# Low parts of the first feed-forward's weights kept in DRAM between the two halves of the sequence

## The chip, the core and the metric

The kernel runs on one NeuronCore of a Trainium2 chip. It is measured in device microseconds per launch. Work is spread over TensorE (PE: matrix products, with PEld its weight loads), VectorE (DVE), ScalarE (ACT), GpSimd (POOL) and SyncE (SP), which here issues nearly all DMAs. Each engine takes its own instructions strictly in order and waits on semaphores of the others.

## The reference

Two layers over 1024 tokens of width 1024, in float32. Layer 0 mixes tokens with attention and pooling, layer 1 with an RWKV-7 recurrence; each is followed by a SwiGLU feed-forward of inner width 2816:

```python
x = x + y                                   # y: the layer's mixer
x = x + (silu(h @ w_gate) * (h @ w_up)) @ w_down   # h = rmsnorm(x)
```

The change concerns only the feed-forward of layer 0 (`w_gate`, `w_up`, `w_down`: 22 blocks of 128 columns each).

## The kernel before

Activations are held transposed, in two halves of 512 tokens. Every float32 weight is split in two: `hi` is the value rounded to the matmul format (a ScalarE copy), `lo = raw - hi` (a VectorE subtract). A product is three matmuls: hi by hi, hi by the activation's lo, lo by hi (`mm3`, lines 163 to 165).

`load_part` (line 142) does this for one part of 128x512 numbers, 256 KB: a DMA on SP into one of two `wraw` buffers (line 150), the copy into `whi` (line 151), the subtract into `wlo` (line 152). `whi` and `wlo` have five buffers each. A raw buffer comes free once its subtract is done, a `whi` or `wlo` buffer once TensorE has used it. So SP's third load waits for the first part's subtract, and ScalarE's sixth copy for the first part's last matmul. One part feeds 12 matmuls of 128x512.

`ffn` (line 683) runs over blocks of 128 inner columns: gate (2 parts), up (2 parts), and behind each group of four blocks the down projection (8 parts, one for each 128 output columns; 4 for the last group of two). One half takes 88 + 44 = 132 parts. A gate's result leaves its PSUM buffer through ScalarE and the VectorE multiply at line 726 (half 1) and an up's at line 732; in half 1 there are two such buffers ("fm").

The layer-0 feed-forward runs once for half 0 (`g0` and line 1367) and once for half 1 (`f1`, line 1369), and each run loads and splits the same weights. In half 0 it stands alone. In half 1 it is filler: 96 matmuls run ahead, and the rest is woven into two `job` calls of the recurrence on half 0. A job first prepares four pairs of heads (many VectorE products into `ZL`, `XR`, `bk`, small matmuls on TensorE), then inverts 32x32 triangles on VectorE alone (30 steps of `pd` and `nu`, lines 1110 and 1112, then transposes of 2 us into `t` and `XR`, lines 1120 and 1118), and then runs eight steps over 64 tokens each. Between these pieces `weave` takes a fixed number of filler matmuls (`rw.fr`: 6, 5, 16, 7, ...), and a scheduler orders every engine's list once, when the program is built. During the jobs SP also loads and stores the recurrence's own tiles (lines 961, 1053, 985).

Of the kernel before, what the change touches and what calls it, by code (L numbers as in the profile page):

```python
# [9 lines left out]
F32 = mybir.dt.float32  # L10
# [6 lines left out]
P = 128  # L17
# [3 lines left out]
HN = 512  # L21
# [59 lines left out]
def rd(ap):  # L81
    return ap.bitcast(F32)


def setup(ctx, tc, k):
    nc = tc.nc
    k.tc, k.nc = tc, nc
    k.const = ctx.enter_context(tc.tile_pool(name="const", bufs=1))
    k.uid = 0
    k.prio, k.cur = {}, 0  # L90
    k.cc = k.const.tile([P, NCC], F32, tag="cc", name="cc")
    k.cv = k.const.tile([P, NCV], F32, tag="cv", name="cv")

    k.eps = k.const.tile([P, 64], F32, tag="eps", name="eps")
    nc.gpsimd.memset(k.eps[:, 0:1], RMS_EPS)
    nc.gpsimd.memset(k.eps[:, 1:2], GN_EPS)
    nc.gpsimd.memset(k.eps[:, 2:3], 1e-35)
    k.hlast = k.const.tile([P, KT], F32, tag="hlast", name="hlast")
    k.om = k.const.tile([P, 48], F32, tag="om", name="om")
    k.nb = k.const.tile([P, 16], F32, tag="nb", name="nb")  # L100
    k.bones = k.const.tile([P, P], F32R, tag="bones", name="bones")
    k.lag2, k.lag3 = 100000, 100000
# [30 lines left out]
    return k.ps.tile([P, HN], F32, tag=tag, name=nm(k, tag), bufs=bufs)  # L133


def load_w(k, ap, tag="w", w=512, bufs=None, pool=None):

    p, n = ap.shape
    return [load_part(k, ap[:, c:c + min(512, n)], p, min(512, n), tag, w, bufs, pool) for c in range(0, n, 512)]


def load_part(k, ap, p, n, tag="w", w=512, bufs=None, pool=None):
    hi, lo = ((pool or k.wp).tile([P, w], F32R, tag=tag + i, name=nm(k, tag + i), bufs=bufs or k.wbufs) for i in ("hi", "lo"))
    raw = k.wp.tile([P, 512], F32, tag="wraw", name=nm(k, "wraw"), bufs=k.rawbufs)
    dst = raw[0:p, 0:n]
    if len(ap.shape) == 3:
        dst = dst.rearrange("p (a b) -> p a b", b=ap.shape[2])
    elif len(ap.shape) == 4:
        dst = dst.rearrange("p (a b c) -> p a b c", b=ap.shape[2], c=ap.shape[3])
    k.nc.sync.dma_start(dst, ap)  # L150
    k.nc.scalar.copy(hi[0:p, 0:n], raw[0:p, 0:n])  # L151
    k.nc.vector.tensor_tensor(lo[0:p, 0:n], raw[0:p, 0:n], rd(hi[0:p, 0:n]), ALU.subtract)  # L152
    return hi, lo


# [34 lines left out]
def run(gen):  # L190

    while True:
        try:
            next(gen)
        except StopIteration as e:
            return e.value


def chain(*gens):
    for g in gens:  # L200
        yield from g
# [478 lines left out]
        out[kt] = part(k, pair(k, *acc), t)  # L680


def ffn(k, ins, L, halves, H, X, acc, tp, groups, after=None, silu=True, fb0=0):
    nc = k.nc

    def project(w):
        o = {half: pmm(k) for half in halves}
        for c in range(2):
            for half in halves:
                yield from mm3(k, o[half], [(blk(w, kt), H[half][kt]) for kt in range(4 * c, 4 * c + 4)], c == 0, c == 1)  # L690
        return o

    def down(n, fb0, acts, last):
        per = max(1, 4 // n)
        cur = None
        for half, m in [(half, m) for half in halves for m in range(8)] if last else [(half, m) for m in range(8) for half in halves]:
            if cur != m // per:
                cur = m // per
                w = []
                for f in range(0, n, 4):  # L700
                    c = min(4, n - f)
                    w.append(load_part(k, ins[f"wd{L}"][per * cur:per * cur + per, :, fb0 + f:fb0 + f + c].rearrange("m p f c -> p m f c"), P, per * c * P))
            o = pmm(k)
            yield from mm3(k, o, [(blk(w, (m % per) * n + i), acts[fb0 + i, half]) for i in range(n)])
            nc.vector.tensor_tensor(X[half][m], o, X[half][m], ALU.add)  # L705
            if last:
                after(half, m)
# [3 lines left out]
    for gi, n in enumerate(groups):  # L711
        acts, sgs = {}, {}
        for fb in range(fb0, fb0 + n):
            g = yield from project(load_w(k, ins[f"wg{L}"][fb]))
            for half in halves:
                sg = sgs[half] = tp.tile([P, HN], F32, tag="nt", name=nm(k, "sg"), bufs=k.ntbufs)
                if silu:
# [8 lines left out]
                    nc.vector.tensor_tensor(sg, g[half], sg, ALU.mult)  # L726
            yield from behind
            behind = iter(())
            u = yield from project(load_w(k, ins[f"wu{L}"][fb]))
            for half in halves:  # L730
                sg = sgs[half]
                nc.vector.tensor_tensor(sg, u[half], sg, ALU.mult)
# [503 lines left out]
def build(ctx, tc, ins, outs, dbg=None, stop=99):  # L1236
    nc = tc.nc
    k = K()
# [5 lines left out]
    H = [[None] * KT for _ in range(2)]  # L1244
    X = [[None] * KT for _ in range(2)]
# [60 lines left out]
    c_m, mp = pool("m1", "right")  # L1306
    c_t, tp = pool("t1", "right")
# [28 lines left out]
    c_u, u = pool("u")  # L1336
# [20 lines left out]

    GP, G0, G1, G2 = ((4,),(),(4,4,4,4,2),(4,4,4,4,2))
    n = sum(GP) + sum(G0)
    g0 = ffn(k, ins, 0, (0,), H, X, U, tp, GP)  # L1360
    ahead(g0, 24)
    for m in MO[1][NP:]:
        on[1].add(X[1][m])
    run(g0)
    make_h(k, on[1], "ffn0", X[1], M, H[1])
    run(ffn(k, ins, 0, (0, 1), H, X, U, tp, G0, fb0=sum(GP)))
    run(ffn(k, ins, 0, (0,), H, X, U, tp, G1, after0, True, n))
    rw.ln_exp, rw.mx, rw.wl_bufs, k.sigm = False, U, 2, True
    f1 = chain(ffn(k, ins, 0, (1,), H, X, M, mp, GP, silu=None), ffn(k, ins, 0, (1,), H, X, M, mp, G2, after0, None, n))
    f1 = using(k, f1, mm=(pf, "fm", 2), ntbufs=3)  # L1370
    lead, share = (96, 0)
    ahead(f1, lead)
# [178 lines left out]
```

## Time and profile before

| | us |
|---|---|
| median of 3 runs | 2699.88 (2699.42 to 2700.76) |
| the profiled execution | 2699.79 |
| its span, first to last instruction | 2698.0 |
| TensorE busy | 2632.5 |
| VectorE busy | 1725.1 |
| ScalarE busy | 1298.7 |

Half 0 of the layer-0 feed-forward lies at about 500 to 850 us, the dense projections of the recurrence at 880 to 1060, the first job at 1060 to 1280 (its VectorE-heavy start until 1180), the second at 1280 to 1500, and the end of the half-1 feed-forward at 1500 to 1560. A 128x512 matmul shows 0.39 us in the trace, but they are pipelined: one starts every 0.22 to 0.23 us. "Idle before" is the time an engine stood still, with the instruction whose end let it go on.

### The profile page before, as it was taken

The numbers are of one execution on the slowest core, as the hardware profiler recorded it, in microseconds if no ns is written. First come the engines' busy times: TensorE is split into PE (matmuls) and PEld (weight loads), VectorE is DVE, ScalarE is ACT, GpSimd is POOL, SyncE is SP. The second block draws the span as 40 slices with busy tenths as digits, with TensorE's granted clock in tenths as the row PEclk, the third lists the DMA queues.
The fourth block names the chain that finished last, engine by engine and source line by source line (L and its number), as shares of the span: only waits on it lengthen the run. The fifth ranks groups of instructions, "written<-read, shape, count | busy, mean of one in ns | idle before, by whom it ended". The sixth has DMA issues, their size and how long they took to land.

```text
span 2698.0 us, 40269 instructions
## 1 busy us (share of the span) xinstructions
PE 2632.5 (98%) x15368; PEld 2072.6 (77%) x15368; DVE 1725.1 (64%) x2940; ACT 1298.7 (48%) x2297; POOL 49.4 (2%) x139
## 2 busy tenths in 40 slices
PE   8999999999999999999999999999999999999999
PEld 6787878788888777777777677777777777888887
DVE  8777684653446655975995676469778856534443
ACT  7555564443224766434634467664445444332232
POOL 1000000000001000000000000000000000000000
PEclk9999999999999999999999999999999999999999
DMA  4111131233333545424433534554244336333333
GB/s 136 58 51 57 42 98 48 83 96 98 96 96 113 172 161 189 129 83 131 148 91 99 195 94 160 168 179 128 87 138 140 92 97 202 101 98 96 97 97 94
DMA packets 170529, 306.11 MB, mean 113 GB/s; under 512 B 18896, under 2 KB 26192, under 8 KB 170336
## 3 DMA queue, kind: packets, MB, share of 16 engines
q1 hardware_dynamic: 156512, 278.38, 33.5%
q10 hardware_dynamic: 13824, 25.17, 2.5%
q8 instruction: 120, 1.97, 0.3%
q14 instruction: 73, 0.60, 0.1%
HBM read 257.04 MB, written 46.43 MB: 112 GB/s over the span
## 4 chain that ended last, share of the span: by engine, by line
PE 77%; DVE 14%; ACT 3%; DMA 3%; issue 3%; SPq 0%; DVEq 0%; ACTq 0%
PE mm L163 16%; PE mm L164 16%; PE mm L165 16%; PE fm L163 6%; PE fm L164 5%; PE fm L165 5%; DVE wlo L152 2%; PE mm L175 1%; DVE nu L1112 1%; DVE pd L1110 1%; DVE ZL L1068 1%; DMA wraw<-in_wd_dram 1%; DMA wraw<-in_wu_dram 1%; ACT whi L151 1%; PE o L1177 1%
## 5 line engine op out<-in xcount | busy, mean ns | idle before, releaser
L151 ACT CAST whi<-wraw 128x512 fp32r<-128x512 f32 x738 | 454.0, 617 | 886.8 <-PE mm L164 484.5
L152 DVE TENSOR_TENSOR wlo<-wraw,whi 128x512 fp32r<-128x512 f32 x738 | 501.3, 683 | 446.0 <-ACT whi L151 436.4
L163 PE MATMUL mm<-hh,whi 128*128 128x512 f32 x864 | 343.7, 400 | 6.7 <-ACT hh L355 6.2
L165 PE MATMUL mm<-hh,wlo 128*128 128x512 f32 x864 | 338.7, 392 | 0.0
L164 PE MATMUL mm<-hl,whi 128*128 128x512 f32 x864 | 337.8, 392 | 0.0
L163 PE MATMUL mm<-uh,whi 128*128 128x512 f32 x728 | 283.5, 391 | 0.9 <-DVE x L1318 0.9
L165 PE MATMUL mm<-uh,wlo 128*128 128x512 f32 x728 | 283.1, 389 | 1.2 <-DVE wlo L152 1.2
L164 PE MATMUL mm<-ul,whi 128*128 128x512 f32 x728 | 283.2, 390 | 0.0
L163 PE MATMUL fm<-h1h,whi 128*128 128x512 f32 x528 | 218.7, 415 | 14.8 <-DVE sg L726 10.6
L165 PE MATMUL fm<-h1h,wlo 128*128 128x512 f32 x528 | 208.7, 396 | 0.5 <-DVE wlo L152 0.5
L164 PE MATMUL fm<-h1l,whi 128*128 128x512 f32 x528 | 208.5, 395 | 0.1
L163 PEld LDWEIGHTS mm<-hh,whi 128*128 128x128 f32 x864 | 162.5, 188 | 43.1 <-ACT hh L355 6.9
L165 PEld LDWEIGHTS mm<-hh,wlo 128*128 128x128 f32 x864 | 162.7, 188 | 34.8 <-DVE wlo L152 0.6
L164 PEld LDWEIGHTS mm<-hl,whi 128*128 128x128 f32 x864 | 162.9, 189 | 32.7 <-DVE hl L260 1.3
L163 PE MATMUL fm<-hh,whi 128*128 128x512 f32 x416 | 172.4, 414 | 3.5 <-ACT hh L259 2.8
L164 PE MATMUL fm<-hl,whi 128*128 128x512 f32 x416 | 164.5, 396 | 0.2 <-DVE hl L260 0.2
L165 PE MATMUL fm<-hh,wlo 128*128 128x512 f32 x416 | 164.6, 396 | 0.0
L163 PEld LDWEIGHTS mm<-uh,whi 128*128 128x128 f32 x728 | 136.5, 188 | 34.6 <-issue 2.7
L164 PEld LDWEIGHTS mm<-ul,whi 128*128 128x128 f32 x728 | 136.6, 188 | 31.1 <-issue 1.1
L165 PEld LDWEIGHTS mm<-uh,wlo 128*128 128x128 f32 x728 | 136.7, 188 | 30.0 <-DVE wlo L152 2.0
L705 DVE TENSOR_TENSOR x<-mm,x 128x512 f32<-128x512 f32 x96 | 66.2, 692 | 119.8 <-PE mm L165 119.6
L163 PEld LDWEIGHTS fm<-h1h,whi 128*128 128x128 f32 x528 | 99.5, 189 | 48.7 <-DVE sg L726 13.3
(338 smaller groups left out, 4632.4 us busy)
## 6 DMA issues: line engine op xcount, KB each, us to landing
wraw<-in_wg_dram SPq DMA_DIRECT2D x176, 256.0 KB, 2.8
wraw<-in_wu_dram SPq DMA_DIRECT2D x176, 256.0 KB, 2.7
wraw<-in_wd_dram SPq DMA_DIRECT2D x176, 256.0 KB, 2.7
wraw<-in_w_in_dram SPq DMA_DIRECT2D x52, 256.0 KB, 2.9
x<-in_xT_dram SPq DMA_DIRECT2D x32, 256.0 KB, 4.8
x<-x SPq DMA_DIRECT2D x32, 256.0 KB, 3.1
wraw<-in_w_k_dram SPq DMA_DIRECT2D x32, 256.0 KB, 2.9
wraw<-in_w_v_dram SPq DMA_DIRECT2D x32, 256.0 KB, 3.0
```

Of the source, the lines that this page charges most:

```text
L151: k.nc.scalar.copy(hi[0:p, 0:n], raw[0:p, 0:n])
L152: k.nc.vector.tensor_tensor(lo[0:p, 0:n], raw[0:p, 0:n], rd(hi[0:p, 0:n]), ALU.subtract)
L163: nc.tensor.matmul(out, wh, xh, start=(first and i == 0), stop=False)
L164: nc.tensor.matmul(out, wh, xl, start=False, stop=False)
L165: nc.tensor.matmul(out, wl, xh, start=False, stop=(last and i == n - 1))
L175: k.nc.tensor.matmul(out[n * q:n * q + n], w[:, n * j:n * j + n], xs[j], start=c == 0, stop=c + g == len(xs), tile_position=(0, n * q))
L705: nc.vector.tensor_tensor(X[half][m], o, X[half][m], ALU.add)
L1068: nc.vector.tensor_tensor(ZL[h][HS[1 - h], i, bs], s4[HS[1]], self.msk[HS[1]].rearrange("p a t -> p (a t)").unsqueeze(1).broadcast_to([64, ...
L1110: nc.vector.tensor_tensor(pv, nu[:, j + 1:32, j:j + 1].broadcast_to([P, n, j]), nu[:, j:j + 1, 0:j].broadcast_to([P, n, j]), ALU.mult)
L1112: nc.vector.tensor_tensor(nu[:, j + 1:32, 0:j], nu[:, j + 1:32, 0:j], pv, ALU.add)
L1177: nc.tensor.matmul(sp[HS[h], i], BK[h][:, i, c], uv[h][:, i], start=True, stop=True)
```

## The change

For the layer-0 feed-forward a part now has a key (layer, matrix, block, column). When half 0 makes a part's `lo`, a DMA on SP stores it in a DRAM tile of its own (new line 160). When half 1 loads the same part, the raw weights still come in and ScalarE still copies `hi`, but `lo` comes by a second DMA on SP from that DRAM tile (new line 155), and no subtract is issued.

```diff
@@ load_w, load_part @@
-    return [load_part(k, ap[:, c:c + min(512, n)], p, min(512, n), tag, w, bufs, pool) for c in range(0, n, 512)]
+    return [load_part(k, ap[:, c:c + min(512, n)], p, min(512, n), tag, w, bufs, pool, key and f"{key}_{c}") for c in range(0, n, 512)]
...
     k.nc.sync.dma_start(dst, ap)
     k.nc.scalar.copy(hi[0:p, 0:n], raw[0:p, 0:n])
+    if key in k.low:
+        k.nc.sync.dma_start(rd(lo[0:p, 0:n]), k.low[key][0:p, 0:n])
+        return hi, lo
     k.nc.vector.tensor_tensor(lo[0:p, 0:n], raw[0:p, 0:n], rd(hi[0:p, 0:n]), ALU.subtract)
+    if key is not None:
+        k.low[key] = k.dram.tile([P, HN], F32, tag="lo" + key, name="lo" + key)
+        k.nc.sync.dma_start(k.low[key][0:p, 0:n], rd(lo[0:p, 0:n]))
     return hi, lo
@@ ffn @@
+    key = lambda *a: "_".join(map(str, (L,) + a)) if keep else None
...
-            g = yield from project(load_w(k, ins[f"wg{L}"][fb]))
+            g = yield from project(load_w(k, ins[f"wg{L}"][fb], key=key("g", fb)))
...
-            u = yield from project(load_w(k, ins[f"wu{L}"][fb]))
+            u = yield from project(load_w(k, ins[f"wu{L}"][fb], key=key("u", fb)))
@@ build @@
-    g0 = ffn(k, ins, 0, (0,), H, X, U, tp, GP)
+    g0 = ffn(k, ins, 0, (0,), H, X, U, tp, GP, keep=True)
...
-    run(ffn(k, ins, 0, (0,), H, X, U, tp, G1, after0, True, n))
+    run(ffn(k, ins, 0, (0,), H, X, U, tp, G1, after0, True, n, True))
...
-    f1 = chain(ffn(k, ins, 0, (1,), H, X, M, mp, GP, silu=None), ffn(k, ins, 0, (1,), H, X, M, mp, G2, after0, None, n))
+    f1 = chain(ffn(k, ins, 0, (1,), H, X, M, mp, GP, silu=None, keep=True), ffn(k, ins, 0, (1,), H, X, M, mp, G2, after0, None, n, True))
```

The down projection's parts get a key ("d") in the same way. Line numbers below the new code grow by 8 to 10. Over the program SP's list grows from 1072 to 1336 rows (132 stores and 132 loads more), VectorE's shrinks by 136, of which 132 are subtracts.

On SP in the middle of half 0, in the third group of blocks, stood only the raw loads, each waiting for a subtract on VectorE (`DVE_49`):

```order
L150 DMA wraw_5665<-in_wu_dram 128x512 [waits DMAHW1_49,DVE_49]
L150 DMA wraw_5671<-in_wu_dram 128x512 [waits DMAHW2_49,DVE_49]
L150 DMA wraw_5707<-in_wg_dram 128x512 [waits DMAHW3_49,DVE_49]
L150 DMA wraw_5713<-in_wg_dram 128x512 [waits DMAHW4_49,DVE_49]
L150 DMA wraw_5746<-in_wd_dram 128x512 [waits DMAHW5_49,DVE_49]
```

In the same place each raw load now has a store of the part two before it ahead of it; the store waits for VectorE, the load for ScalarE's copy:

```order
L152 DMA wraw_5741<-in_wu_dram 128x512 [waits DMAHW4_49,Activation_49]
L160 DMA lo_g_512_5710<-wlo_5705 128x512 [waits DMAHW1_49,DVE_49]
L152 DMA wraw_5749<-in_wu_dram 128x512 [waits DMAHW6_49,Activation_49]
L160 DMA lo_u_0_5745<-wlo_5740 128x512 [waits DMAHW3_49,DVE_49]
L152 DMA wraw_5787<-in_wg_dram 128x512 [waits DMAHW0_49,Activation_49]
L160 DMA lo_u_512_5753<-wlo_5748 128x512 [waits DMAHW5_49,DVE_49]
L152 DMA wraw_5795<-in_wg_dram 128x512 [waits DMAHW2_49,Activation_49]
L160 DMA lo_g_0_5791<-wlo_5786 128x512 [waits DMAHW7_49,DVE_49]
```

Since the store of a part comes ahead of the load two parts later on the same queue, that load still comes after the same subtract.

On VectorE at the end of the triangles of the first job (`nu`, `pd`: the inversion; `t`, `XR`: its transposes; `sg`, `h1l`: the filler's results) stood:

```order
L152 TENSOR_TENSOR wlo_10632<-wraw_10633,whi_10631 128x512
L1112 TENSOR_TENSOR nu_10220<-nu_10220,pd_10595 128x2x29
L260 TENSOR_TENSOR h1l_10519<-sg_10460,h1h_10518 128x512
L1110 TENSOR_TENSOR pd_10604<-nu_10220 128x30
L1112 TENSOR_TENSOR nu_10220<-nu_10220,pd_10604 128x30
L1120 STREAM_TRANSPOSE t_2458_10613<-nu_10220 128x32x32
L1118 STREAM_TRANSPOSE XR_9420<-nu_10220 32x32x32 x2
L152 TENSOR_TENSOR wlo_10638<-wraw_10639,whi_10637 128x512
L152 TENSOR_TENSOR wlo_10745<-wraw_10746,whi_10744 128x512
L1118 STREAM_TRANSPOSE XR_9420<-nu_10220 32x32x32
L726 TENSOR_TENSOR sg_10574<-fm_10534,sg_10574 128x512
L1118 STREAM_TRANSPOSE XR_9420<-nu_10220 32x32x32
```

Now it reads (line numbers 10 higher there):

```order
L1122 TENSOR_TENSOR nu_10484<-nu_10484,pd_10859 128x2x29
L1120 TENSOR_TENSOR pd_10868<-nu_10484 128x30
L1122 TENSOR_TENSOR nu_10484<-nu_10484,pd_10868 128x30
L1130 STREAM_TRANSPOSE t_2458_10877<-nu_10484 128x32x32
L1128 STREAM_TRANSPOSE XR_9684<-nu_10484 32x32x32
L736 TENSOR_TENSOR sg_10724<-fm_10687,sg_10724 128x512
L1128 STREAM_TRANSPOSE XR_9684<-nu_10484 32x32x32 x3
L742 TENSOR_TENSOR sg_10724<-fm_10741,sg_10724 128x512
L268 TENSOR_TENSOR h1l_10783<-sg_10724,h1h_10782 128x512
L736 TENSOR_TENSOR sg_10838<-fm_10798,sg_10838 128x512
```

The three subtracts are gone from it, and the transposes stand one block of the feed-forward earlier against the filler: `sg_10838` now is what `sg_10574` was, and comes behind the transposes, not between them.

On SP at the start of the first job (`ld`: the recurrence's tiles) the loads of `lo` now stand between the job's own, waiting for TensorE (`PE_49`) to be done with the part five before; before, that place had raw loads that wait for VectorE:

```order
L150 DMA wraw_9718<-in_wu_dram 128x512 [waits DMAHW6_49,DVE_49]
L150 DMA wraw_9792<-in_wd_dram 128x512 [waits DMAHW7_49,DVE_49]
L961 DMA ld_9674<-a_0_8592 128x512 [waits DMAHW0_49,DVE_49]
L1053 DMA c_0_9497<-ld_9490 128x512 [waits DMAHW1_49,DVE_49]
L961 DMA ld_9683<-r_0_9030 128x512 [waits DMAHW2_49,DMAHW1_49]
```

```order
L155 DMA wlo_9975<-lo_u_0_5160 128x512 [waits DMAHW1_49,PE_49]
L155 DMA wlo_9981<-lo_u_512_5168 128x512 [waits DMAHW2_49,PE_49]
L152 DMA wraw_10056<-in_wd_dram 128x512 [waits DMAHW3_49,Activation_49]
L155 DMA wlo_10055<-lo_d_0_5206 128x512 [waits DMAHW4_49,PE_49]
L971 DMA ld_9938<-a_0_8856 128x512 [waits DMAHW5_49,DVE_49]
L152 DMA wraw_10097<-in_wd_dram 128x512 [waits DMAHW6_49]
```

Two to three loads of `lo` now stand ahead of the load of `a` there.

## Rows read from the trace of the kernel before

**Rows 1.** the page, part 1 (busy us, share of the span, instructions)
```profile
PE 2632.5 (98%) x15368; PEld 2072.6 (77%) x15368; DVE 1725.1 (64%) x2940; ACT 1298.7 (48%) x2297; POOL 49.4 (2%) x139
```

**Rows 2.** the page, part 4, the chain that ended last, shares by engine
```profile
PE 77%; DVE 14%; ACT 3%; DMA 3%; issue 3%; SPq 0%; DVEq 0%; ACTq 0%
```

**Rows 3.** windows by stage: start:end, length, busy us of each engine, clock, DMA, GB/s
```profile
500.00:850.00 350.00, 350.00 (x1542) 288.94 (x1541) 159.63 (x243) 121.81 (x198) 0.00 (x0) 1.00 0.34 100
...
1060.00:1180.00 120.00, 109.94 (x799) 85.72 (x800) 111.83 (x193) 60.74 (x111) 3.69 (x12) 0.99 0.39 120
...
1180.00:1280.00 100.00, 100.00 (x1058) 73.87 (x1057) 58.16 (x103) 44.53 (x89) 1.31 (x4) 1.00 0.36 113
...
1280.00:1400.00 120.00, 111.86 (x754) 87.49 (x753) 114.34 (x198) 61.03 (x110) 3.89 (x14) 0.99 0.41 127
...
1500.00:1560.00 60.00, 54.22 (x220) 41.28 (x219) 44.38 (x71) 25.85 (x44) 0.00 (x0) 0.97 0.61 205
```

**Rows 4.** TensorE's waits, 1060 to 1180 us (us in total, times, longest)
```profile
PE fm L163 <- DVE sg L726: 5.7, 3, 4.1
...
PE s L1060 <- DVE ZL L1068: 2.5, 3, 1.0
```

**Rows 5.** TensorE's waits, 1280 to 1400 us
```profile
PE fm L163 <- DVE sg L726: 4.5, 2, 2.8
...
PE s L1060 <- DVE ZL L1068: 1.1, 1, 1.1
...
PE s L1060 <- DVE bk L1044: 1.0, 1, 1.0
```

**Rows 6.** VectorE lines, 1060 to 1180 us (busy us, mean ns, idle before)
```profile
L152 DVE TENSOR_TENSOR wlo<-wraw,whi 128x512 fp32r<-128x512 f32 x32 | 21.7, 686 | 1.6 <-ACT whi L151 1.4
...
L1118 DVE STREAM_TRANSPOSE XR<-nu 32x1024 f32<-32x1024 f32 x4 | 7.9, 1971 | 0.1
```

**Rows 7.** VectorE line, 1280 to 1400 us
```profile
L152 DVE TENSOR_TENSOR wlo<-wraw,whi 128x512 fp32r<-128x512 f32 x31 | 20.9, 685 | 0.4
```

**Rows 8.** windows of 20 us around the two low clocks, columns of Rows 3
```profile
1160.00:1180.00 20.00, 15.94 (x181) 12.39 (x180) 15.62 (x16) 7.92 (x14) 0.00 (x0) 0.91 0.23 67
...
1380.00:1400.00 20.00, 17.21 (x127) 13.64 (x126) 19.36 (x33) 4.61 (x8) 0.00 (x0) 0.91 0.27 79
```

**Rows 9.** TensorE's waits, 870 to 1060 us
```profile
PE mm L165 <- DVE wlo L152: 1.2, 1, 1.2
```

**Rows 10.** TensorE's waits, 1500 to 1560 us
```profile
PE fm L307 <- DVE sq L302: 2.6, 1, 2.6
```

**Rows 11.** DMA issues, 640 to 840 us (KB each, median us to landing)
```profile
wraw<-in_wg_dram SPq DMA_DIRECT2D x23, 256.0 KB, 2.9
```

**Rows 12.** timeline in half 0 (start us, us, engine; idle before in brackets)
```profile
642.28 3.05 SPq L150 DMA_DIRECT2D wraw<-in_wg_dram  x2
...
643.62 0.62 ACT L151 CAST whi<-wraw 128x512 fp32r<-128x512 f32 x1 [1.60 <-PE mm L164]
...
644.28 0.69 DVE L152 TENSOR_TENSOR wlo<-wraw,whi 128x512 fp32r<-128x512 f32 x1 [2.03 <-ACT whi L151]
...
646.35 0.62 ACT L151 CAST whi<-wraw 128x512 fp32r<-128x512 f32 x1 [2.10 <-PE mm L164]
```

**Rows 13.** timeline, back-to-back loads on SP
```profile
1514.34 1.57 SPq L1392 DMA_DIRECT2D y<-y  x3
```

**Rows 14.** DMA issues, 900 to 1040 us
```profile
wraw<-in_w_v_dram SPq DMA_DIRECT2D x16, 256.0 KB, 3.0
...
a<-ev ACTq DMA_DIRECT2D x8, 256.0 KB, 3.7
```

**Rows 15.** VectorE line, 500 to 853 us
```profile
L152 DVE TENSOR_TENSOR wlo<-wraw,whi 128x512 fp32r<-128x512 f32 x129 | 88.6, 688 | 101.7 <-ACT whi L151 101.5
```

**Rows 16.** DMA issues, 1500 to 1550 us
```profile
wraw<-in_wd_dram SPq DMA_DIRECT2D x4, 256.0 KB, 4.1
...
y<-y SPq DMA_DIRECT2D x8, 256.0 KB, 3.9
```

More of the change, by code (lines that the diff above doesn't have):

```diff
@@ L90, in setup @@
     k.prio, k.cur = {}, 0
+    k.low = {}
     k.cc = k.const.tile([P, NCC], F32, tag="cc", name="cc")
@@ L133, in pst, with load_w, load_part @@
     return k.ps.tile([P, HN], F32, tag=tag, name=nm(k, tag), bufs=bufs)
-def load_w(k, ap, tag="w", w=512, bufs=None, pool=None):
+def load_w(k, ap, tag="w", w=512, bufs=None, pool=None, key=None):
     p, n = ap.shape
-    return [load_part(k, ap[:, c:c + min(512, n)], p, min(512, n), tag, w, bufs, pool) for c in range(0, n, 512)]
-def load_part(k, ap, p, n, tag="w", w=512, bufs=None, pool=None):
+    return [load_part(k, ap[:, c:c + min(512, n)], p, min(512, n), tag, w, bufs, pool, key and f"{key}_{c}") for c in range(0, n, 512)]
+def load_part(k, ap, p, n, tag="w", w=512, bufs=None, pool=None, key=None):
     hi, lo = ((pool or k.wp).tile([P, w], F32R, tag=tag + i, name=nm(k, tag + i), bufs=bufs or k.wbufs) for i in ("hi", "lo"))
@@ L680, in make_h, with ffn @@
         out[kt] = part(k, pair(k, *acc), t)
-def ffn(k, ins, L, halves, H, X, acc, tp, groups, after=None, silu=True, fb0=0):
+def ffn(k, ins, L, halves, H, X, acc, tp, groups, after=None, silu=True, fb0=0, keep=False):
     nc = k.nc
+    key = lambda *a: "_".join(map(str, (L,) + a)) if keep else None
     def project(w):
@@ L701, in down @@
                     c = min(4, n - f)
-                    w.append(load_part(k, ins[f"wd{L}"][per * cur:per * cur + per, :, fb0 + f:fb0 + f + c].rearrange("m p f c -> p m f c"), P, per * c * P))
+                    w.append(load_part(k, ins[f"wd{L}"][per * cur:per * cur + per, :, fb0 + f:fb0 + f + c].rearrange("m p f c -> p m f c"), P, per * c * P,
+                                       key=key("d", cur, fb0 + f)))
             o = pmm(k)
```

## The prediction

> **What bounds the kernel now.** I read the page's busy times first, then the chain that ended last, then windows by stage, and in the stages that the change touches the waits of TensorE, the lines of VectorE and a timeline. The busy times show TensorE at 98% of the span and VectorE at 64% [rows 1], so work taken from VectorE is worth something only where TensorE stands still for it. The chain of waits says that there are such places: 77% of it runs through TensorE, 14% through VectorE [rows 2]. The windows by stage say where [rows 3]. In half 0 of the layer-0 feed-forward (500 to 850 us) TensorE is busy all of the 350 us and VectorE less than half of them. In the VectorE-heavy start of each of the two jobs, which half 1 fills, it is the other way round: VectorE is busy 111.8 and 114.3 of 120 us, TensorE 109.9 and 111.9. Between and after these (1180 to 1280 us, for one) TensorE is full again. So TensorE is idle 120 - 109.94 = 10.06 us in the first such stretch and 120 - 111.86 = 8.14 us in the second, 18.2 us together. The waits there name VectorE: the filler's matmuls stand for the gate's multiply at line 726, which must free a PSUM buffer (5.7 and 4.5 us), and the job's own for `ZL` (2.5 and 1.1 us) and `bk` (1.0 us) [rows 4, 5].
>
> **What the change removes.** Half 1 has 132 parts, so 132 subtracts go, at 0.686 us each [rows 6] 90.6 us of VectorE's time. What counts is the share inside the two stretches: 32 and 31 subtracts, 21.7 and 20.9 us [rows 6, 7]. Without them VectorE has 111.8 - 21.7 = 90.1 us and 114.3 - 20.9 = 93.4 us to do, TensorE still 109.9 and 111.9. TensorE becomes the bound there, and the most that can be had is its idle 18.2 us. I take that the waits for line 726 and the small ones go, since they come of a VectorE that is late with everything, and that the waits for `ZL` and `bk`, 2.5 + 1.1 + 1.0 = 4.6 us, stay, since they are a chain of products from one engine to the next. That leaves 18.2 - 4.6 = 13.6 us.
>
> The two longest waits (4.1 and 2.8 us [rows 4, 5]) also cost clock: in the 20 us around each the granted clock is 0.91 [rows 8], 0.09 x 20 = 1.8 us lost, 3.6 us together. Before each drop TensorE had stood still once for so long, and it got the full clock back after a few us of matmuls. If the waits go, I count these 3.6 us as well: 17.2 us.
>
> Outside of the two stretches I count nothing. The subtracts in the jobs' later parts and in the lead before the first job lie beside a full TensorE. Bounds there: the dense projections' first wait for a `lo`, 1.2 us [rows 9], may go since eight subtracts of the lead stand ahead of it; the 2.6 us at the end of half 1 [rows 10] come of a chain of norm products, and could shrink at most by themselves.
>
> **What it adds in half 0.** There are 132 stores of 256 KB on SP, each waiting for its subtract, with the raw loads queued behind. The load of part n+2 stands behind the store of part n, and it had to wait for subtract n already, to get its raw buffer. So the wait itself is nothing new; what is new is SP's time for one more DMA and the company on the DMA engines. A raw buffer's round is now: 2.9 us to landing [rows 11], 0.62 us copy, 0.69 us subtract [rows 12], some 0.1 us of handing over, 4.3 us. It may take two parts' time, as there are two buffers; copies follow each other at 643.62 and 646.35 [rows 12], so that is 2 x 2.73 = 5.46 us. Both copies waited for TensorE, not for a load: the cover is 1.15 us. One more issue on SP takes up to (1.57 - 0.33)/2 = 0.62 us, by three loads issued one behind another, with 0.33 us for the last [rows 13]. The company doubles the traffic from 100 GB/s [rows 3] to 200. In the dense projections loads of the same size, with stores of 256 KB among them, landed in 3.0 us [rows 14], 0.1 us later. 4.3 + 0.62 + 0.1 = 5.0 us is under 5.46: I count 0. VectorE does not get slower by it: its 129 subtracts there [rows 15] stay as they are. The stores' landing holds a `wlo` buffer, 3.7 us for the slowest kind shown [rows 14], and it is wanted again only five parts, 13.6 us, later.
>
> The bounds: below, nothing can be gained, since TensorE is full; above, a transfer of 256 KB takes 0.262 MB / 100 GB/s x 0.34 = 0.89 us of all 16 engines [rows 3], and if the load behind waited for all of it the round would be 4.3 + 0.62 + 0.89 = 5.8 us, 0.35 us too long for two parts, over 129 parts 0.35 x 129 / 2 = 23 us. I take 0, by the row of the mixed traffic, which is the nearest.
>
> The Trainium skill speaks for the upper bound, page "DMA: Bandwidth & Descriptors", section "Queues, rings and completion order": SP owns one ring on each DMA engine, and "on each SDMA engine descriptors are consumed in ring order". By that rule every load would start only behind the store's packets. The dense projections' stores came from ScalarE's queue, so no row here has a store and a load on one ring back to back; by the rule alone it is the slower rival below.
>
> **What it adds in half 1.** There are 132 more loads of 256 KB on SP. A `lo` load waits until TensorE is done with the part five before. The subtract that it replaces had the same wait through ScalarE's copy, so its data come at 2.9 us instead of 0.62 + 0.69 = 1.3 us after that point, and are wanted four parts or at least 10.9 us after it. The raw buffer now comes free one subtract earlier. What stands behind a waiting `lo` load is the job's own loads. At the start of the first job the load of `a` stands about two parts later against the filler than before, 24 matmuls or 2 x 2.73 = 5.5 us. It is fetched a whole pair of heads ahead, so I count 0. Bounds: below, up to 2.6 us at the end of half 1; above, 5 us at the end of half 1, where loads already land in 4.1 and 3.9 us [rows 16] at 205 GB/s [rows 3].
>
> **Sum.** 2699.8 us (the profiled execution, 0.1 us from the median; its span and 1.8 us around it) - 13.6 - 3.6 = 2682.6, or 2683 us.
>
> **Rivals.** (A) The wait moves. On VectorE three transposes into `XR` now stand in a row, 3 x 1.97 us [rows 6], with the up's multiply and the next block's behind them. If TensorE comes there early, it stands again, as it did for 4.1 and 2.8 us, and loses the clock again: 6.9 + 3.6 = 10.5 us of the gain stay away, 2693 us, or somewhat more if smaller waits stay too. For it: the old waits lie just at these transposes. Against it: the transposes now stand one block, 48 matmuls or 10.9 us, earlier against the filler. (B) Slower: half 0 becomes bound by its loads. Place: SP, each raw load behind a store. Price: 23 us on top of the forecast, 2706 us. It decides once the round exceeds 5.46 us, which is once store and traffic add more than 1.15 us. Against it: the 3.0 us of the mixed traffic; for it: the ring rule. (C) The `lo` loads hold back the jobs' loads, and VectorE starts each of eight pairs of heads late by half of the 5.5 us: 8 x 2.7 = 22 us, less what the filler hides, with the 17 us gained about 2699 us. (D) All of the idle time goes, with the clock and the waits in the bounds: 18.2 + 3.6 + 1.2 + 2.6 = 25.6 us, 2674 us. That the change would not take the subtracts off is excluded by VectorE's list.
>
> **How the numbers follow.** What counts as no change is 0.2%, 5.4 us, about what a measurement of this kernel can tell. Forecast 0.62 (2677 to 2690 us), D 0.10, A 0.13, C 0.07, B 0.08. Faster (under 2694.5 us): 0.62 + 0.10 and half of A, 0.78. Same: the other half of A and most of C, 0.13. Slower: B and a rest of C, 0.09. The range from 2674 to 2702 us leaves out B and what lies beyond D.
>
> **What would show it.** Right: in the two VectorE-heavy stretches TensorE's windows are full, the waits for line 726 (736 now) are under 2 us in all, the clock is 1.00 there, the stretches are together some 17 us shorter, and half 0 takes its 350 us with ScalarE's copies still waiting for TensorE. Wrong: copies in half 0 that wait for a raw load (B), TensorE waiting behind the transposes (A), VectorE waiting for `ld` loads in the jobs' first 60 us (C), or TensorE waiting for a `wlo` DMA.

## The result: 0.35% slower, where 0.6% faster was forecast

| | kernel before | kernel after |
|---|---|---|
| median, us (6 runs each) | 2699.65 (2698.15 to 2700.76) | 2708.94 (2704.66 to 2714.88) |
| profiled execution, us; its span | 2699.79; 2698.0 | 2710.91; 2708.6 |
| mean granted clock in it | 0.996 | 0.993 |

The ratio is 1.0035, 95% interval 1.0023 to 1.0048. The forecast was 2683 us, the range 2674 to 2702 us, with a chance of 0.09 for slower. VectorE did lose its work, and TensorE did not get shorter by it. The page of the kernel after, busy times and the chain's shares (they answer to [rows 1, 2]):

```profile
PE 2638.7 (97%) x15368; PEld 2080.0 (77%) x15368; DVE 1647.1 (61%) x2808; ACT 1296.6 (48%) x2297; POOL 46.7 (2%) x139
...
PE 75%; DVE 14%; DMA 5%; ACT 4%; issue 2%; SPq 0%; ACTq 0%; DVEq 0%
```

VectorE has 132 instructions less, the subtracts. Its busy time fell by 1725.1 - 1647.1 = 78.0 us, less than their 90.6 us, since the records of neighbours overlap in the trace. Its share of the chain stayed 14%, and DMA's rose from 3 to 5%. The windows by stage (columns as in [rows 3]):

```profile
500.00:850.00 350.00, 348.61 (x1532) 286.75 (x1531) 156.70 (x239) 119.99 (x196) 0.00 (x0) 1.00 0.61 194
1060.00:1180.00 120.00, 112.33 (x811) 89.21 (x810) 98.14 (x166) 61.84 (x114) 3.78 (x13) 0.97 0.60 190
...
1280.00:1400.00 120.00, 109.64 (x726) 86.24 (x727) 98.89 (x169) 61.74 (x112) 3.99 (x15) 0.94 0.61 190
1500.00:1560.00 60.00, 53.83 (x208) 40.01 (x208) 32.13 (x50) 24.20 (x42) 0.00 (x0) 0.94 0.75 253
```

In the two job starts VectorE has 13.7 and 15.5 us less to do than before, but TensorE's idle time went from 10.1 to 7.7 us in the first and from 8.1 to 10.4 us in the second: 18.0 us in place of 18.2. The clock is lower in both (0.97 and 0.94, before 0.99 and 0.99), and at the end of half 1, the last row (0.94, before 0.97). TensorE's waits in these two stretches, the first two rows from 1060 to 1180 us, the others from 1280 to 1400 us (they answer to [rows 4, 5]):

```profile
PE fm L171 <- DVE sg L736: 3.4, 2, 2.4
PE s L1070 <- DVE ZL L1078: 2.7, 2, 1.5
...
PE fm L171 <- DVE sg L736: 7.2, 2, 6.2
PE s L1070 <- ACT XR L1075: 1.4, 1, 1.4
```

One wait of 6.2 us is new, longer than any of the job starts before (4.1). VectorE's list at that place, of the kernel after (start us, us, engine, line):

```profile
1382.67 2.26 DVE L1130 STREAM_TRANSPOSE t<-nu 128x1024 f32<-128x1024 f32 x1
1384.96 7.69 DVE L1128 STREAM_TRANSPOSE XR<-nu 32x1024 f32<-32x1024 f32 x4
1392.69 0.69 DVE L736 TENSOR_TENSOR sg<-fm,sg 128x512 f32<-128x512 f32 x1
```

and TensorE's row that waits for the last of these:

```profile
1393.43 0.80 PE L171 MATMUL fm<-h1h,whi 128*128 128x512 f32 x1 [6.21 <-DVE sg L736]
```

All five transposes, 2.26 + 7.69 = 9.95 us, stand ahead of the multiply that frees the filler's PSUM buffer. That is rival A's mechanism, at one place, and the wait is 6.2 us where A put 2.8 us for this job.

**Where TensorE stands still, by the job's steps.** The windows by time compare different work. These go by what VectorE does: the chain of products of the first pairs (from the job's first `t` matmul to the first `pd`), the triangles (`pd`, `nu`), and the five transposes; first job, then second. The kernel before:

```profile
1053.70:1125.00 71.30, 66.81 (x501) 50.89 (x501) 69.40 (x104) 42.85 (x79) 3.46 (x7) 1.00 0.45 144
1125.00:1158.40 33.40, 31.78 (x139) 25.54 (x138) 31.48 (x83) 15.52 (x27) 0.75 (x6) 1.00 0.35 105
1158.40:1170.30 11.90, 7.84 (x32) 6.09 (x31) 11.78 (x8) 3.62 (x6) 0.00 (x0) 0.91 0.21 65
1278.20:1355.10 76.90, 73.29 (x534) 56.15 (x533) 73.06 (x110) 45.99 (x84) 3.89 (x14) 1.00 0.48 151
1355.10:1388.70 33.60, 29.07 (x123) 23.29 (x122) 31.90 (x84) 14.43 (x25) 0.00 (x0) 0.97 0.36 104
1388.70:1402.10 13.40, 13.40 (x116) 10.92 (x115) 13.23 (x11) 3.07 (x5) 0.00 (x0) 0.95 0.16 54
```

The kernel after:

```profile
1057.80:1128.70 70.90, 66.65 (x501) 52.45 (x502) 61.34 (x90) 44.75 (x85) 3.03 (x7) 0.98 0.67 215
1128.70:1153.70 25.00, 23.97 (x105) 19.21 (x104) 23.04 (x68) 10.90 (x19) 0.75 (x6) 1.00 0.58 186
1153.70:1164.60 10.90, 8.45 (x30) 6.47 (x30) 10.78 (x6) 0.81 (x2) 0.00 (x0) 0.84 0.35 107
1279.90:1356.60 76.70, 73.67 (x525) 57.50 (x525) 62.94 (x93) 47.22 (x87) 3.24 (x9) 0.96 0.68 218
1356.60:1382.60 26.00, 24.89 (x109) 19.99 (x108) 24.11 (x69) 10.98 (x19) 0.75 (x6) 1.00 0.61 181
1382.60:1392.60 10.00, 4.62 (x78) 3.65 (x76) 9.89 (x6) 3.01 (x5) 0.00 (x0) 0.95 0.48 138
```

TensorE's idle time is each row's length less its busy time:

| idle of TensorE, us (first + second job) | before | after |
|---|---|---|
| products | 4.5 + 3.6 | 4.3 + 3.0 |
| triangles | 1.6 + 4.5 | 1.0 + 1.1 |
| transposes | 4.1 + 0.0 | 2.5 + 5.4 |
| sum | 18.3 | 17.3 |

This table is the answer to why the freed VectorE was worth nothing. The triangles are bound by VectorE, and they got 33.4 + 33.6 - 25.0 - 26.0 = 16.0 us shorter. But TensorE was busy there for most of the time, with the filler, and what it does not do in a shorter stretch it must do later: its busy time there fell by (31.78 + 29.07) - (23.97 + 24.89) = 12.0 us, 139 + 123 - 105 - 109 = 48 matmuls fewer. Only the other 4.0 us were idle time. The products' idle time hardly moved, though VectorE now rests 9.6 and 13.8 us there: it comes of a chain from engine to engine, not of VectorE's load. And the transposes took 3.8 of the 4.0 us back (from 4.1 to 7.8). Outside of these rows a wait of 1.7 us for `kn` now lies just ahead of the first job's (1056.1 us).

### The profile page after: what moved, and what is told of

Read it like the earlier page. It is cut to its first block, busy times and chain, and to the rows that moved or that the text cites. A ratio compares the mean times of both kernels' runs of the same rounds, so it can differ in the third digit from the quotient of the medians.

```text
span 2708.6 us, 40601 instructions
## 1 busy us (share of the span) xinstructions
PE 2638.7 (97%) x15368; PEld 2080.0 (77%) x15368; DVE 1647.1 (61%) x2808; ACT 1296.6 (48%) x2297; POOL 46.7 (2%) x139
## 4 chain that ended last, share of the span: by engine, by line
PE 75%; DVE 14%; DMA 5%; ACT 4%; issue 2%; SPq 0%; ACTq 0%; DVEq 0%
PE mm L171 15%; PE mm L172 15%; PE mm L173 15%; PE fm L171 6%; PE fm L172 6%; PE fm L173 5%; DVE wlo L157 2%; DVE nu L1122 1%; DVE pd L1120 1%; PE mm L183 1%; DMA wraw<-in_wu_dram 1%; DVE ZL L1078 1%; ACT whi L153 1%; DMA wraw<-in_wg_dram 1%; PE o L1187 1%
## 5 line engine op out<-in xcount | busy, mean ns | idle before, releaser
L157 DVE TENSOR_TENSOR wlo<-wraw,whi 128x512 fp32r<-128x512 f32 (+1 forms) x606 | 411.2, 682 | 422.6 <-ACT whi L153 363.4
L171 PE MATMUL fm<-h1h,whi 128*128 128x512 f32 x528 | 222.0, 421 | 16.8 <-DVE sg L736 10.6
```

The lines of the kernel that those rows point to most:

```text
L171: nc.tensor.matmul(out, wh, xh, start=(first and i == 0), stop=False)
```

## The experiments

"Before" is the kernel before in the same series, from 27 to 34 runs; its medians were 2700.51 (the first four kernels), 2701.14 (the next four), 2702.94 (the four with a lead of 120) and 2703.22 us (the last three). Since each run also reports its mean granted clock, I split each time: clock loss = 2700 us x (1 - mean clock over the runs), the rest = mean time less that. Both are given as differences to before in the same series; over the 11 or 12 runs of a kernel (5 of e12) the rest is good to some 2 us (95%), the clock loss to 2 or 3 us. Time at the low clock in which TensorE stands counts as clock loss, so the split can put a little too much on the clock. Names: O is the theory that the order of VectorE's list keeps the gain away, D that the DMA traffic does.

| kernel | median us | ratio to before, 95% | rest, us | clock loss, us |
|---|---|---|---|---|
| e1 stores alone | 2704.28 | 1.0011 [1.0002, 1.0020] | +3.3 | +0.5 |
| e2 loads in half 1 alone | 2706.89 | 1.0020 [1.0011, 1.0029] | -0.4 | +5.9 |
| e3 no subtract, no DMA | 2700.57 | 1.0005 [0.9996, 1.0013] | -4.1 | +5.9 |
| e5 after, two transposes held | 2702.93 | 1.0009 [0.9999, 1.0020] | +0.9 | +1.5 |
| e6 e3, two transposes held | 2696.69 | 0.9983 [0.9974, 0.9992] | -5.6 | +2.3 |
| e8 before, two transposes held | 2697.24 | 0.9990 [0.9982, 0.9999] | -1.2 | -1.4 |
| e7 e5, stores from GpSimd | 2705.31 | 1.0011 [1.0001, 1.0020] | -0.6 | +3.7 |
| e9 e5, more filler | 2708.29 | 1.0026 [1.0018, 1.0035] | +0.4 | +7.0 |
| e10 after, lead 120 | 2708.23 | 1.0018 [1.0009, 1.0026] | +2.8 | +2.0 |
| e11 e10, stores from GpSimd | 2708.55 | 1.0019 [1.0007, 1.0030] | +1.2 | +3.9 |
| e12 e11, 6 matmuls a step | 2712.08 | 1.0035 [1.0022, 1.0047] | +5.0 | +4.3 |
| e13 before, lead 120 | 2699.47 | 0.9989 [0.9980, 0.9998] | +0.4 | -3.4 |
| e14 e1, stores later | 2706.01 | 1.0010 [1.0002, 1.0019] | +3.7 | -1.2 |
| e15 e5, stores later | 2708.75 | 1.0015 [1.0004, 1.0025] | +1.0 | +3.0 |
| e16 before, held and lead 120 | 2700.63 | 0.9992 [0.9983, 1.0001] | +0.7 | -2.6 |

**The change in two halves, e1 and e2.** e1 keeps half 0's stores, and half 1 subtracts as before:

```diff
-    f1 = chain(ffn(..., GP, silu=None, keep=True), ffn(..., G2, after0, None, n, True))
+    f1 = chain(ffn(..., GP, silu=None), ffn(..., G2, after0, None, n))
```

> Only half 0's 132 stores are kept; half 1 makes its low parts by subtracts as before. Theory O (order: the freed VectorE's list puts four 2 us transposes in a row ahead of the filler's gate multiply, TensorE stands behind them and its clock drops) expects the time of before plus the 2.4 us that half 0 lost in the changed kernel: 2702 us. Theory D (DMA: the doubled traffic on SP and the DMA engines makes loads late, in half 0 and half 1) expects about the same here, 2702 to 2704 us, since half 0 has half of the new transfers.

e2 stores only the first four `lo` and lets half 1 load these in turn, so its list of loads is that of the kernel after and half 0 is free of all but four stores:

```diff
+        i = len(k.low)
+        if i < 4:
             ...
+        else:
+            k.low[key] = list(k.low.values())[i % 4]
```

> Only half 1's 132 loads, without the stores: four low parts are stored in half 0, and half 1 reads these four in turn (so its products use the wrong low parts), with no subtracts. The lists of all engines in half 1 are those of the changed kernel. Theory O: the changed kernel less half 0's loss, 2709 - 2.4 = 2706 to 2707 us, with the 6.2 us wait at the second job's transposes. Theory D: likewise 2706 to 2707 us, the loss being in the loads of half 1; this run says how the loss is shared between the halves.

Both halves lose: mean times 3.8 us (e1) and 5.5 us (e2) over before, together 9.2 of the 9.7 us between the means of after and before. e1's loss lies in the rest, e2's in the clock; e2 has the 6.2 us wait of the kernel after at the same place. The steps of the table above repeat: in e1, which subtracts, the triangles take 33.2 and 33.3 us and TensorE stands 18.2 us over the six rows, as before; in e2, which does not, 25.0 and 26.0 us and 17.1 us, as after.

**The freed VectorE alone, e3.** Neither subtract nor DMA in half 1, no stores; half 1 uses its high part in place of the low one:

```diff
     if key in k.low:
-        k.nc.sync.dma_start(rd(lo[0:p, 0:n]), k.low[key][0:p, 0:n])
-        return hi, lo
+        return hi, hi
```

> Half 1 has neither subtracts nor loads of low parts: its third product uses the high part twice, so the low part of the weights is left out, and half 0 stores nothing. VectorE is freed and there is no added DMA. Theory O: VectorE's list has the same four transposes in a row, so TensorE stands there still; no gain worth naming, 2700 to 2706 us. Theory D: the gain that I forecast appears, 2683 us.

Even with the subtracts gone for nothing the kernel is not faster. Steps as above, of this kernel:

```profile
1050.60:1123.20 72.60, 66.58 (x503) 52.19 (x502) 62.01 (x92) 44.62 (x84) 3.03 (x7) 0.98 0.47 153
1123.20:1148.20 25.00, 23.99 (x105) 19.20 (x104) 23.08 (x67) 10.46 (x19) 0.75 (x6) 1.00 0.27 93
1148.20:1159.70 11.50, 9.02 (x33) 6.95 (x32) 11.35 (x8) 2.11 (x4) 0.00 (x0) 0.85 0.17 50
1274.70:1348.50 73.80, 70.60 (x521) 54.70 (x521) 62.55 (x93) 46.03 (x85) 3.20 (x8) 1.00 0.50 160
1348.50:1374.40 25.90, 24.99 (x109) 20.00 (x108) 24.05 (x69) 10.76 (x19) 0.75 (x6) 1.00 0.30 92
1374.40:1384.40 10.00, 4.55 (x57) 3.53 (x55) 9.90 (x7) 2.89 (x5) 0.00 (x0) 0.90 0.29 80
```

The triangles take the same 25.0 and 25.9 us, the transposes cost 2.5 + 5.5 us of idle time (with the 6.2 us wait), and the sum over the six rows is 19.1 us, more than before's 18.3. This kernel bounds the prediction's first two steps by themselves: -4.1 us of rest and +5.9 us of clock, where -13.6 and -3.6 us were forecast. So the missing gain is not D's doing; D's share is the loss on top of it. The loads cost another 3.6 us (mean of e2 less that of e3, 5.46 - 1.82; 95% interval 1.2 to 6.1).

**The order of the transposes: e5, e6, e8.** In the first half's jobs two of the four transposes into `XR` are made to follow VectorE's first copy of `g`, so that the filler's multiplies come between:

```diff
+            if q in (0, 2) and half == 0:
+                k.tc.add_manual_dep(i.ins, held.ins.name, ..., reason="behind")
...
-                copy_to(k, "AV"[ci], g[qs], gps[qs])
+                if ci and half == 0 and b == 0:
+                    held = nc.vector.tensor_copy(g[qs], gps[qs])
```

e5 does it to the kernel after, e6 to e3, e8 to the kernel before.

> The changed kernel with the last two of the four transposes of each half-0 job held behind VectorE's first copy of g, so that the gate's multiply is not behind them. Theory O: the 6.2 us wait becomes under 3 us and the 6.8 us at half clock behind it becomes 3.4 or none, so 2709 - 5 to 7 = 2702 to 2704 us. Theory D: 2708 to 2710 us as the changed kernel.

> This joins two edits already measured apart: no store, no load and no subtract of low parts (half 1 uses its high part twice; the low part is left out), 2700.6 us, and two of the four transposes of the first half's jobs held behind VectorE's first copy of g, which took 6.0 us off the changed kernel (2708.9 to 2702.9). Theory O (the order on VectorE ate the gain of the freed VectorE): the 6.2 us wait for line 736 at about 1380 us shrinks to about 3 us, the half clock behind it from 6.8 to 3.4 us, and the time is 2700.6 - 3.2 - 1.7 to 2700.6 - 6.0, so 2694.6 to 2695.7 us. Theory D (all of the loss is the DMA traffic; the transposes don't matter without it): 2700 to 2701 us, and the wait stays or comes back elsewhere.

> A control: the kernel before, with its subtracts and without any DMA of low parts, and the same two transposes held back. Theory O: in the kernel before, the gate's multiply already stands between the transposes, so holding two of them is worth the rest of its 4.1 and 2.8 us waits at most: 2697 to 2700.5 us. If the holding is instead worth the same 6 us anywhere, it has nothing to do with the change: 2694 us.

In e5 the 6.2 us wait is halved (TensorE's wait, 1280 to 1410 us, of e5):

```profile
PE fm L171 <- DVE sg L736: 4.0, 2, 3.0
```

By the medians e5 takes 6.0 us off the kernel after and e6 3.9 us off e3 (each from two series), e8 3.9 us off before (0.1% by its ratio). So the order is worth something once the subtracts are gone, but not only then. e6, with all of the change's benefit and none of its DMA, stands 0.17% or 4.5 us under before: that is what was to be had at best with this order, and the part of it that does not come from the change (e8, 3.9 us) is more than half by the medians, though the intervals of the two overlap. e8 lies under both kernels; its interval just leaves 1 out.

**More filler and another phase: e9, e10, e12, e13.** e9 adds 5 matmuls at each of three places among the transposes to e5; e10 runs 120 in place of 96 matmuls ahead of the dense projections, which by the engines' lists was to put the multiply behind the second transpose in both jobs; e12 is e10 with the stores of e11 and 6 in place of 5 matmuls a triangle step; e13 is before with a lead of 120.

```diff
-        yield self.fr[half][2]
+        yield self.fr[half][2] + (0 if half else 5)
...
-    lead, share = (96, 0)
+    lead, share = (120, 0)
...
-    rw.fr = [6, 6, 5, 16, 7, 9, 16], ...
+    rw.fr = [6, 6, 6, 16, 7, 9, 16], ...
```

> The changed kernel with two transposes held, and in the first half's jobs 5 more matmuls' worth of filler after the transposes of t11 and after the first two into XR (3 places in each of two jobs; later places get that much less). Theory O: the 2.96 us wait that is left at 1383 us is covered by 15 x 0.228 = 3.4 us more of filler there, and the half clock behind it (3.4 us) goes as well: 2702.9 - 3.0 - 1.7 = 2698 us. If the filler runs into the same wait for line 736 since its PSUM buffer is held: no change, 2703 us.

> The changed kernel with one number altered: 120 instead of 96 matmuls of half 1's filler run ahead of the dense projections. By the lists this shifts the blocks of the filler against the jobs by half a block: the gate's multiply (line 736) comes behind the second of five transposes in both jobs, where in the changed kernel it came behind the third in the first job and behind all five in the second. No transpose is held. Theory O (only the place of that multiply among the transposes): the 6.2 us wait at about 1384 us goes to 2 to 3 us, as when two transposes were held, the half clock behind it halves, and the time is about that of the held ones, 2701 to 2704 us. Theory W (VectorE has too much to do in that stretch, wherever the multiply stands): the wait only moves to another place of the stretch, idle time between 1285 and 1410 us stays at 10 us, 2707 to 2710 us.

> The same again, with 6 instead of 5 matmuls of filler for each step of the triangles and transposes in the first half's jobs (some 36 steps in each of two jobs). TensorE stands 7 to 8 us in each of the two stretches since the filler there is shorter than VectorE's work. Theory O2 (more filler in the triangles covers it): the waits for line 736 fall under 3 us together in each stretch, 2696 to 2699 us. Theory W2 (each block of filler brings VectorE work of its own and holds the same PSUM buffer): as with 5, or slower by the end of half 1, where the filler then runs out earlier: 2702 to 2708 us.

> A control: the kernel before (with its subtracts, without any DMA of low parts) with the same lead of 120. If the place of the multiply among the transposes is what counts, this kernel, which had it between them already, gains nothing: 2699 to 2703 us. If a lead of 120 is better for any kernel, for another reason: 2695 us.

In e10's trace the multiply stands behind the second transpose in the second job only (1394.15 us). In the first it stands behind all five (1170.33 us), and TensorE waits 3.4 us there, so e10's time alone does not judge my narrow theory, that only the place of that one multiply counts. The second job does. TensorE waits only 2.0 us for the multiply from 1280 to 1410 us, but other waits took its place (TensorE's waits there, of e10), and over that job's three steps it stands 9.6 us, 9.5 in the kernel after:

```profile
PE s L1140 <- DVE t L1130: 2.7, 1, 2.7
PE fm L171 <- DVE sg L736: 2.0, 2, 1.3
```

With the multiply early, TensorE comes to the job's own matmul, which needs the transposes, and stands there. More filler at the place does not cover it either: e9's waits for the multiply come to 5.1 us with one of 3.7, and a wait of 2.8 us for `kn` is new; e12 is the slowest of all. These were all misses of mine. What they share: no placement tried brought the two stretches' idle time far down. Over the same six steps, to the last transpose, it is 14.7 us in e5, 15.6 in e6, 15.9 in e10, 18.0 in e12 and 18.8 in e9, of 18.3 before, while VectorE's ten microseconds of transposes stand against some 15 matmuls of filler.

**Half 0: e7, e11, e14, e15.** e7 and e11 issue the stores from GpSimd's queue; e14 and e15 issue each one part later, so that on SP the raw load now stands ahead of the store:

```diff
-        k.nc.sync.dma_start(k.low[key][0:p, 0:n], rd(lo[0:p, 0:n]))
+        k.nc.gpsimd.dma_start(k.low[key][0:p, 0:n], rd(lo[0:p, 0:n]))
...
+        k.late.append((k.low[key][0:p, 0:n], rd(lo[0:p, 0:n])))
+        if len(k.late) > 2:
+            k.nc.sync.dma_start(*k.late.pop(0))
```

> The changed kernel with two transposes held (2702.9 us), and the 132 stores of half 0 issued from GpSimd's queue in place of SP's. Theory D1 (half 0's loss comes of stores standing between the raw loads on SP's one queue): raw loads land in 2.6 to 2.7 us again, the loss of 2.4 us in half 0 goes, about 2700.5 us. Theory D2 (the loss comes of the doubled traffic on the DMA engines, from whatever queue): loads stay at 2.8 to 3.0 us and the time at 2703 us. If GpSimd's issuing slows VectorE's subtracts: over 2704 us.

> The same with half 0's stores issued from GpSimd's queue. From the earlier pair (2.4 us lost in half 0 with stores on SP's queue, 1.4 with GpSimd's): 1 us under the kernel with the lead alone, 2700 to 2703 us. If the queue doesn't matter for the whole: the same as that one.

> Half 0's stores alone (half 1 subtracts as the kernel before does), as in the earlier run that took 2704.3 us and lost some 2.4 us in half 0, but each store is issued one part later: on SP the raw load of part n now stands ahead of the store of part n - 2 and waits for nothing but its own buffer. Theory Q (half 0 loses since each raw load stands behind a store in SP's order): loads land in 2.6 to 2.7 us again, half 0 loses under 0.5 us, the whole 2700 to 2702 us. Theory T (the doubled traffic slows whatever moves, in any order): loads at 2.8 to 3.0 us, the loss of 2 to 2.5 us stays, 2704 us.

> The whole change with the later stores and with two of the first half's transposes held behind the first copy of g (the held version took 2702.9 us with the early stores). Theory Q: 2.4 us less, 2700 to 2701 us, level with the kernel before. Theory T: 2703 us.

From the first `mm<-uh` matmul to the filler's first one half 0 takes 360.6 us before, 363.0 after, 363.0 in e5, 362.0 in e7 and 363.2 in e14. So another queue gave back 1.0 of 2.4 us and the other order nothing: the theory that the order on SP's queue costs the time fell. As a whole e7 and e11 missed what I expected, too: e7's 2705.31 us is above e5, with half 0's subtracts at 689 ns, not slower than e5's 690, a better rest and more clock loss; e11 is level with e10. ScalarE's waits for raw loads, 560 to 850 us, of before:

```profile
ACT whi L151 <- DMA wraw<-in_wg_dram: 7.9, 5, 2.5
...
ACT whi L151 <- DMA wraw<-in_wu_dram: 5.0, 4, 2.3
...
ACT whi L151 <- DMA wraw<-in_wd_dram: 1.4, 1, 1.4
```

and of after:

```profile
ACT whi L153 <- DMA wraw<-in_wg_dram: 28.6, 14, 4.0
ACT whi L153 <- DMA wraw<-in_wu_dram: 24.6, 12, 4.7
ACT whi L153 <- DMA wraw<-in_wd_dram: 17.3, 10, 2.8
```

Copies wait for loads 10 times and 36 times in these rows, and 39 times in e14 (16, 13 and 10, for 30.1, 24.9 and 16.8 us). Which of them pass on to TensorE is seen at 530 to 540 us (ScalarE, kernel after):

```profile
535.68 0.62 ACT L153 CAST whi<-wraw 128x512 fp32r<-128x512 f32 x1 [1.19 <-DMA wraw<-in_wd_dram]
538.13 0.62 ACT L153 CAST whi<-wraw 128x512 fp32r<-128x512 f32 x1 [1.83 <-DMA wraw<-in_wd_dram]
540.12 0.62 ACT L267 CAST uh<-sg 128x512 fp32r<-128x512 f32 x1 [1.36 <-DVE sg L742]
```

The copy at 538.13 comes as soon as its load lands; on VectorE its subtract (538.79) stands ahead of the multiply for `sg` (539.40), which has long been wanted, and the copy to `uh` follows at 540.12; TensorE stood 1.28 us. Before, that multiply was at 536.65, ahead of its neighbour's subtract. A late load costs little by itself; it costs by what is queued behind its copy and its subtract. Set against the kernel before matmul by matmul, half 0 of the kernel after falls behind in two places only: here, by 1.7 us (the stall and a slow start behind it), and at 592 us, by 0.7 us, behind the copy that had waited 4.7 us for its load of `wu`. None of the other late copies held up a matmul: of the 36 above, 35 cost nothing. In e7 and e14 only the first place is left, with 1.4 and 2.6 us. What part the doubled traffic has in this (0.61 of the DMA engines' time in place of 0.34) no run isolates.

**Both known losses mended, e15, and e16.**

> The kernel before with two transposes held and with the lead of 120, which alone gave ratios of 0.9990 and 0.9989. If both take the same stalls away: 0.999 again, 2698 to 2700 us. If they add up: 0.998, 2696 us. It tells whether the order of this stretch, which the change disturbs, is worth as much without the change as the change was thought to bring.

e15 is not level with before (1.0015, its interval from 1.0004 up), and the two orders in e16 do not add up (0.9992). No version with the whole change beats the kernel before.

## Why the prediction was wrong

- **Step 1, the waits in the job starts: this step failed.** It took all waits but those for `ZL` and `bk` as "a VectorE that is late with everything", 13.6 us. The traces show three causes in three steps. Where VectorE's volume did bind, in the triangles, idle time fell by 4.0 us, and most of the subtracts' time turned into a shorter stretch with fewer matmuls in it. Of the two longest waits the 2.8 us one lay there as well, ahead of the transposes, and it went (the kernel before):

```profile
1385.93 0.50 PE L163 MATMUL fm<-h1h,whi 128*128 128x512 f32 x1 [2.79 <-DVE sg L726]
...
1388.69 2.17 DVE L1120 STREAM_TRANSPOSE t<-nu 128x1024 f32<-128x1024 f32 x1
```

  The 4.1 us one belonged to the transposes, a block of 10 us in which only two subtracts, 1.3 us, stood ahead of the multiply; there the idle time rose by 3.8 us. The error in the working was to set VectorE's and TensorE's busy times of 120 us against each other, as if TensorE could use any freed moment of VectorE.
- **Step 2, the clock: wrong in sign.** 3.6 us were to come back. The clock loss grew instead: 0.004 x 2698.0 = 10.8 us in the profiled execution before, 0.007 x 2708.6 = 19.0 us after. Over the runs the growth is smaller: the six runs of the kernel after have a mean clock of 0.993, 18.9 us, and the kernel before loses 13.5 to 15.7 us in the four later series.
- **Step 3, half 0 at nothing: too low by 2.4 us,** within the bounds given (0 to 23 us). The round of a raw buffer was well sized: copies that wait for loads follow each other at 2.45 us (535.68, 538.13), 4.9 us for two parts against the 5.0 forecast. What I left out is that a part whose cover is small delays its neighbours through two in-order engines. The loads of `wg` from 560 to 850 us landed in 2.7 us before (first row) and in 3.0 us after (second row):

```profile
wraw<-in_wg_dram SPq DMA_DIRECT2D x34, 256.0 KB, 2.7
...
wraw<-in_wg_dram SPq DMA_DIRECT2D x35, 256.0 KB, 3.0
```

  So rival B's sign came, copies that wait for a raw load, but half 0 did not become bound by its loads: B came at a tenth of its price. The rule that I cited for it stands in the Trainium skill, page "DMA: Bandwidth & Descriptors", section "Queues, rings and completion order": descriptors on one ring are consumed in ring order. By it every load would start behind the store's packets; the trace shows loads 0.3 us later, a third of the 0.89 us that the upper bound took for this, and does not tell whether that comes of the order or of the traffic. Taking the load ahead of the store, in e14, made the loads no faster (3.0 to 3.4 us) and the half no shorter.
- **Step 4, half 1's loads at nothing: too low by some 3.6 us** (e2 against e3). At the end of half 1 [rows 10, 16] loads were late and stood ahead of other work; TensorE's waits from 1500 to 1560 us after:

```profile
PE fm L171 <- DVE x L715: 3.2, 3, 2.3
PE fm L171 <- ACT h1h L267: 1.9, 1, 1.9
```

  The first is there without the loads, too (e3: 3.1 us, the longest 2.3). The second is not in e3; it is ScalarE's copy `h1h` at 1546.12 behind two `whi` copies that waited for loads (rows of ScalarE):

```profile
1543.57 0.62 ACT L153 CAST whi<-wraw 128x512 fp32r<-128x512 f32 x1 [1.74 <-DMA wraw<-in_wd_dram]
1545.59 0.62 ACT L153 CAST whi<-wraw 128x512 fp32r<-128x512 f32 x1 [1.40 <-DMA wraw<-in_w_o_dram]
1546.12 0.61 ACT L267 CAST h1h<-sg 128x512 fp32r<-128x512 f32 x1
```

  That was the bound of "above, 5 us at the end of half 1". The 1.2 us wait of the dense projections [rows 9] did go, as its bound said, and the wait of 1.7 us for `kn` came; e3 has it too (1.7 us), so it is not the loads' doing. These waits account for only a part of the 3.6 us.
- **Rival A** named the right mechanism, with a chance of 0.13 and a price that left the kernel faster: it had the wait as long as the old ones, in place of the whole block of transposes, and no loss from the DMAs beside it. Its reason that the old waits lie just at the transposes held for the 4.1 us alone.
- **Rival C** did not come: VectorE's waits for `ld` loads from 1060 to 1120 us are 0.6 us in all, and the products take 70.9 + 76.7 us, 71.3 + 76.9 before.

The ledger, in means: e3 gives -4.1 + 5.9 = +1.8 us for the freed VectorE, the loads +3.6 us, the stores +3.8 us (e1), together 9.2 of 9.7 us, if they add; each is good to 2 or 3 us.

**What stays open.** Why the clock loss grows. The ten kernels whose half 1 does not subtract have more of it than before, by 1.5 to 7.0 us; the five that subtract have not (-3.4 to +0.5 us). It is not the DMA (e3, e6). TensorE's idle time in these stretches is nearly the same; its stalls lie elsewhere. In the two profiled executions the growth lies in the two job starts and the end of half 1. Open, too, is which kernel order would have turned the freed VectorE into time: e6, the best, got 4.5 of the 17.2 us forecast.

## What to carry to other kernels

Freeing an engine that is busy 95% of a stretch is worth the idle time that the bound engine has inside that stretch for want of it, and no more: split the stretch by what the engine does there, and ask of each piece what its filler will do if the piece gets shorter. Work that is taken off also moves what is left: print the new order around long instructions that cannot be interleaved and add up what now stands in one row ahead of a buffer's release. A prefetch with a microsecond of cover is not free on in-order engines, since a late arrival delays whatever is queued behind its copy; here two late copies did, and cost all of half 0's 2.4 us.

## What was not expected of the hardware

A short stall can cost more by the clock than by itself. After the 6.2 us wait the granted clock was 0.50 (of the two levels the lower, 1.2 GHz) for 6.8 us, 5.0 of them with TensorE at work; but so it was after a stall of 1.4 us. Windows of the kernel after, each stall and the stretch at the lower level behind it:

```profile
1291.06:1292.50 1.44, 0.04 (x1) 0.01 (x1) 1.40 (x4) 1.39 (x5) 0.20 (x1) 1.00 0.95 253
1292.60:1299.40 6.80, 6.80 (x49) 5.42 (x49) 5.84 (x10) 3.64 (x8) 0.00 (x0) 0.50 0.49 169
1387.20:1391.60 4.40, 0.02 (x1) 0.00 (x0) 4.37 (x3) 0.00 (x0) 0.00 (x0) 1.00 0.38 117
1391.60:1398.40 6.80, 4.97 (x12) 3.90 (x13) 2.35 (x3) 0.00 (x0) 0.00 (x0) 0.50 0.00 0
```

In the second row TensorE is busy for all of 6.8 us at half speed, so the 1.4 us stall cost 3.4 us more. The kernel before had stalls of 1.74 and 1.66 us at which it kept the full clock (windows of before):

```profile
1362.00:1366.00 4.00, 2.26 (x11) 1.84 (x11) 3.82 (x10) 1.76 (x4) 0.00 (x0) 1.00 0.35 107
1503.90:1508.00 4.10, 2.44 (x11) 1.99 (x11) 3.99 (x7) 0.51 (x1) 0.00 (x0) 1.00 0.34 128
```

It kept it also behind the 2.7 us wait at 2047.2 us (1.00 from 2049.9 to 2060 us). So a stall's length does not tell alone whether the clock falls, and a ledger of such a kernel needs the clock as a term of its own: the two profiled executions differ by 11.1 us, 8.2 of it by the mean clock.
